# The tail of a ReLU-mean kernel: other column pieces, a third partial sum, and waits in another order

## The chip, the cores and the metric

One core of one Trainium2 chip runs the program. The metric is the time of one execution in device microseconds, the lower the better. Times are medians of several executions of the same program; the profile is of one execution, and its span, from the first to the last instruction, is about 1.3 us shorter than the timed run.

## The reference

```python
x = randn(32, 512, 1024) as float32
out = mean(maximum(x, 0), axis=-1)        # (32, 512) float32
```

That is 16,384 rows of 1024 numbers: 67 MB to read, 64 KB to write. ReLU with a sum along the row is one instruction per 128 rows on either VectorE or ScalarE.

## The kernel before

All loads are issued by SyncE, in the order in which they are used. The first 128 rows go apart, then 7 loads of 8 MB rotate through three buffers, then come row pieces of 7, 4, 2 and 1 rows per partition. The very last row of each partition is cut into column pieces, so that work on it can start before all of it is there. The two helpers are one instruction each in the program; in the profile each shows as an operation followed by a read of the accumulator.

```python
def act_row(nc, src, acc):                       # ScalarE
    return nc.scalar.activation(out=src, in_=src, func=ACT.Relu, accum_out=acc)

def dve_row(nc, src, acc, init=None):            # VectorE
    return nc.vector.tensor_scalar(out=src, in0=src, scalar1=0.0, scalar2=init,
                                   op0=ALU.max, op1=ALU.add, accum_out=acc)
# ...
    col_pieces = [512, 256, 256]
    last = sbuf("last", P, D + 2)                # the last row, and two partial sums behind it
    scale = sbuf("scale", P, D // 4 + 2)         # filled with 1/D
# ...
    nc.scalar.wait_ge(loaded[i + 1], 16)         # first piece
    act_row(nc, last[:, :512], last[:, D:D + 1]).then_inc(act, 1)
    nc.vector.wait_ge(loaded[i + 2], 16)         # second piece
    dve_row(nc, last[:, 512:768], last[:, D + 1:D + 2]).then_inc(dve, 1)
    nc.vector.wait_ge(act, n_done + 1)
    nc.vector.wait_ge(dve, n_done + 1)
    nc.vector.wait_ge(loaded[i + 3], 16)         # third piece
    nc.vector.scalar_tensor_tensor(              # "the final operation"
        out=last[:, 768:], in0=last[:, 768:], scalar=0.0, in1=scale[:, :],
        op0=ALU.max, op1=ALU.mult, accum_out=res[:, J - 1:J],
    ).then_inc(dve, 1)

    nc.sync.wait_ge(pool, 2)
    nc.sync.wait_ge(dve, n_done + 2)
    nc.sync.dma_start(out=outr, in_=res[:, :]).then_inc(stored, 16)   # "the store"
```

The final operation reads the third piece and, in the same pass, the two partial sums that stand behind it in memory. A partial sum is never negative, so the ReLU leaves it alone, and one multiplication by 1/D and one accumulation give the mean. It therefore waits for three things: the third load, ScalarE's count and VectorE's own count.

In the built program each of these instructions carries one wait. Where there are more, the others go to an EventSemaphore instruction set ahead of it, which holds up to two. Which wait goes where follows from the order of the calls. With two or three waits the one called first stays in the instruction, and those called later go to the EventSemaphore, the last call at its head. For the final operation above this gives [third load, VectorE] in the EventSemaphore and ScalarE in the instruction.

## Time and profile before

| | before |
|---|---|
| median of 3 runs, then of 6 | 161.53 us, 161.47 us (161.30 to 161.75) |
| packets of the load queue, share of 16 engines' span | 97.7% |
| VectorE busy, ScalarE busy | 46%, 44% |
| final operation starts, after the last count of the third load | 0.240 us |
| store starts, after the last count of the third load | 0.750 us |
| last count of the store, after its start | 1.639 us |

The first rows say that the kernel is a stream of loads with two engines that keep up easily. The last three say what is not covered by the stream: the tail. The last rows are worked out from the semaphore records in the trace, which hold the time of each increment. A load or store raises its semaphore in 16 steps of one; "landed" is the last of the 16. An engine's count is the increment that an operation makes at its end.

### The profile page before, as it was taken

The numbers are of one execution on the slowest core, as the hardware profiler recorded it, in microseconds if no ns is written. First come the engines' busy times: TensorE is split into PE (matmuls) and PEld (weight loads), VectorE is DVE, ScalarE is ACT, GpSimd is POOL, SyncE is SP. The second block draws the span as 40 slices with busy tenths as digits, with TensorE's granted clock in tenths as the row PEclk, the third lists the DMA queues.
The fourth block names the chain that finished last, engine by engine and source line by source line (L and its number), as shares of the span: only waits on it lengthen the run. The fifth ranks groups of instructions, "written<-read, shape, count | busy, mean of one in ns | idle before, by whom it ended". The sixth has DMA issues, their size and how long they took to land. (4 is left out here: it accounts for less than half of the span.)

```text
span 160.2 us, 347 instructions
## 1 busy us (share of the span) xinstructions
DVE 73.3 (46%) x131; ACT 70.4 (44%) x133; POOL 1.3 (1%) x9
## 2 busy tenths in 40 slices
DVE  0000029900498006960079500993009920299984
ACT  1400029800496006950079300991009900299983
POOL 1000000000000000000000000000000000000001
DMA  9969969979989899699699699699699797998992
GB/s 393 507 278 523 507 278 523 442 344 523 409 376 523 360 425 524 294 491 523 262 524 523 262 523 524 262 523 523 262 524 458 327 523 327 425 451 367 419 412 102
DMA packets 2312, 67.18 MB, mean 419 GB/s; under 512 B 392, under 2 KB 648, under 8 KB 1032
## 3 DMA queue, kind: packets, MB, share of 16 engines
q1 hardware_dynamic: 2312, 67.18, 97.7%
HBM read 67.11 MB, written 0.07 MB: 419 GB/s over the span
## 5 line engine op out<-in xcount | busy, mean ns | idle before, releaser
L20 DVE TENSOR_SCALAR_CACHE_REDUCE rows<-rows 128x1024 f32<-128x1024 f32 (+1 forms) x63 | 72.1, 1208 | 78.9 <-DMA rows<-in_x_dram 78.7
L15 ACT ACTIVATE rows<-rows 128x1024 f32<-128x1024 f32 x64 | 66.2, 1035 | 84.1 <-DMA rows<-in_x_dram 83.9
L15 ACT ACTIVATION_READ_ACCUMULATOR rows<-rows 128x1 f32 x64 | 11.9, 186 | 0.0
L20 DVE DVE_READ_ACCUMULATOR rows<-rows 128x1 f32 x63 | 5.2, 82 | 0.0
L168 DVE STREAM_TRANSPOSE turned<-mean 128x32 f32<-128x32 f32 x1 | 0.2, 213 | 5.9 <-ACT row L164 5.9
L164 ACT ACT_TABLE_LOAD x1 | 1.3, 1283 | 3.3 <-DMA row<-in_x_dram 3.3
L157 POOL TENSOR_SCALAR res<-sums 128x112 f32<-128x112 f32 (+1 forms) x2 | 0.5, 250 | 154.0 <-DVE rows L20 154.0
L164 ACT ACTIVATE row<-row 128x1024 f32<-128x1024 f32 x1 | 1.1, 1056 | 0.0
L15 ACT ACTIVATE last<-last 128x512 f32<-128x512 f32 x1 | 0.6, 630 | 0.0
L20 DVE TENSOR_SCALAR_CACHE_REDUCE last<-last 128x256 f32<-128x256 f32 x1 | 0.4, 420 | 0.3 <-DMA last<-in_x_dram 0.3
L197 DVE SCALAR_TENSOR_TENSOR last<-last,scale 128x258 f32<-128x258 f32 x1 | 0.4, 428 | 0.1
L142 POOL MEMSET scale<- 128x258 f32 x1 | 0.3, 314 | 0.0
L187 POOL TENSOR_SCALAR res<-part 128x1 f32<-128x1 f32 x1 | 0.3, 267 | 0.6 <-DVE rows L20 0.6
L164 ACT ACTIVATION_READ_ACCUMULATOR row<-row 128x1 f32 x1 | 0.2, 186 | 0.0
L15 ACT ACTIVATION_READ_ACCUMULATOR last<-last 128x1 f32 x1 | 0.2, 186 | 0.0
L141 POOL MEMSET mean<- 128x32 f32 x1 | 0.1, 126 | 1.5 <-POOLq L55 1.5
L232 POOL MEMSET const-uint8-127<- 128x1 uint8 x1 | 0.1, 103 | 0.0
L232 POOL MEMSET const-bfloat16-1.0<- 128x1 bf16 x1 | 0.1, 102 | 0.0
L232 POOL MEMSET const-float32-0.0<- 128x1 f32 x1 | 0.1, 99 | 0.2 <-issue 0.2
L232 POOL MEMSET const-float32-1.0<- 128x1 f32 x1 | 0.1, 99 | 0.0
L20 DVE DVE_READ_ACCUMULATOR last<-last 128x1 f32 x1 | 0.1, 83 | 0.0
L197 DVE DVE_READ_ACCUMULATOR last<-last,scale 128x1 f32 x1 | 0.1, 82 | 0.0
## 6 DMA issues: line engine op xcount, KB each, us to landing
rows<-in_x_dram SPq DMA_DIRECT2D x1, 3584.0 KB, 38.1
rows<-in_x_dram SPq DMA_DIRECT2D x1, 2048.0 KB, 42.6
rows<-in_x_dram SPq DMA_DIRECT2D x1, 1024.0 KB, 44.7
row<-in_x_dram SPq DMA_DIRECT2D x1, 512.0 KB, 3.3
rows<-in_x_dram SPq DMA_DIRECT2D x1, 512.0 KB, 45.4
last<-in_x_dram SPq DMA_DIRECT2D x1, 256.0 KB, 45.6
last<-in_x_dram SPq DMA_DIRECT2D x2, 128.0 KB, 45.4
rows<-in_x_dram SPq DMA_DIRECT2D x7, 48.8
```

The costliest lines, as they stand in the source:

```text
L15: return nc.scalar.activation(out=src, in_=src, func=ACT.Relu, accum_out=acc)
L20: return nc.vector.tensor_scalar(out=src, in0=src, scalar1=0.0, scalar2=init, op0=ALU.max, op1=ALU.add, accum_out=acc,)
L141: nc.gpsimd.memset(mean0[:, :], 0.0)
L142: nc.gpsimd.memset(scale[:, :], inv).then_inc(pool, 1)
L157: nc.gpsimd.tensor_scalar(out=res[:, lo:hi], in0=sums[:, lo:hi], scalar1=inv, scalar2=0.0, op0=ALU.mult, op1=ALU.add,)
L164: nc.scalar.activation(out=row0[:, :], in_=row0[:, :], func=ACT.Relu, scale=inv, accum_out=mean0[:, 0:1],).then_inc(first, 1)
L168: nc.vector.transpose(turned0[:, :], mean0[:, :]).then_inc(first, 1)
L187: nc.gpsimd.tensor_scalar(out=res[:, J - 2:J - 1], in0=part[:, 0:1], scalar1=part[:, 1:2], scalar2=inv, op0=ALU.add, op1=ALU.mult,).then_i ...
L197: nc.vector.scalar_tensor_tensor(out=last[:, 768:], in0=last[:, 768:], scalar=0.0, in1=scale[:, :], op0=ALU.max, op1=ALU.mult, accum_out=r ...
L232: nc = _bacc.Bacc("TRN2", target_bir_lowering=False, num_devices=1)
```

## The change

Its intent has two parts. VectorE sat idle for 0.29 us between the row before and the second piece; by making the first piece larger (576) and the second smaller (192), and giving VectorE 128 columns of the first, it is to work in that time and be done sooner. And the wait that passes last is to stand in the instruction itself, so that no EventSemaphore has to run after it.

```diff
-    col_pieces = [512, 256, 256]
+    col_pieces = [576, 192, 256]
-    last = sbuf("last", P, D + 2)
-    scale = sbuf("scale", P, D // 4 + 2)
+    last = sbuf("last", P, D + 3)
+    scale = sbuf("scale", P, D // 4 + 3)
...
-    act_row(nc, last[:, :512], last[:, D:D + 1]).then_inc(act, 1)
+    act_row(nc, last[:, :448], last[:, D:D + 1]).then_inc(act, 1)
+    nc.vector.wait_ge(loaded[i + 1], 16)
+    dve_row(nc, last[:, 448:576], last[:, D + 1:D + 2])
     nc.vector.wait_ge(loaded[i + 2], 16)
-    dve_row(nc, last[:, 512:768], last[:, D + 1:D + 2]).then_inc(dve, 1)
-    nc.vector.wait_ge(act, n_done + 1)
+    dve_row(nc, last[:, 576:768], last[:, D + 2:D + 3]).then_inc(dve, 1)
     nc.vector.wait_ge(dve, n_done + 1)
     nc.vector.wait_ge(loaded[i + 3], 16)
+    nc.vector.wait_ge(act, n_done + 1)
     nc.vector.scalar_tensor_tensor(
...
+    nc.sync.wait_ge(dve, n_done + 2)
     nc.sync.wait_ge(pool, 2)
-    nc.sync.wait_ge(dve, n_done + 2)
     nc.sync.dma_start(out=outr, in_=res[:, :]).then_inc(stored, 16)
```

In the built program the final operation now has [ScalarE, third load] in its EventSemaphore, and VectorE's own count in the instruction. The store has GpSimd's count in the EventSemaphore and the final operation's count in itself.

## The prediction

> **What bounds the kernel now.** I read the page's slices first, then the chain that ended last, then the timeline of the last four microseconds, then short windows over its DMA.
>
> ```profile
> span 160.2 us, 347 instructions
> DVE 73.3 (46%) x131; ACT 70.4 (44%) x133; POOL 1.3 (1%) x9
> DMA  9969969979989899699699699699699797998992
> q1 hardware_dynamic: 2312, 67.18, 97.7%
> ```
>
> The queue's packets fill 97.7% of what 16 engines had; VectorE and ScalarE work under half of the span. The body is the load of 67 MB and nothing in the diff touches its size or the seven large loads. Only the tail after the last bytes can change, and the chain that ended last sees only that tail:
>
> ```profile
> 157.97 0.09 issue
> 158.06 0.12 DVE last L197
> 158.18 0.24 issue
> 158.41 0.08 DVE last L197
> ```
>
> L197 is the final operation on VectorE, and ahead of it stand 0.09 us in which nothing works. The timeline (start, length, engine, line) tells how the tail got there:
>
> ```profile
> 156.49 0.58 ACT L15 ACTIVATE rows<-rows 128x448 f32<-128x448 f32 x1
> 156.49 0.75 DVE L20 TENSOR_SCALAR_CACHE_REDUCE rows<-rows 128x576 f32<-128x576 f32 x1
> 157.16 0.63 ACT L15 ACTIVATE last<-last 128x512 f32<-128x512 f32 x1
> 157.17 0.08 DVE L20 DVE_READ_ACCUMULATOR rows<-rows 128x1 f32 x1
> 157.54 0.42 DVE L20 TENSOR_SCALAR_CACHE_REDUCE last<-last 128x256 f32<-128x256 f32 x1 [0.29 <-DMA last<-in_x_dram]
> 157.70 0.19 ACT L15 ACTIVATION_READ_ACCUMULATOR last<-last 128x1 f32 x1
> 157.89 0.08 DVE L20 DVE_READ_ACCUMULATOR last<-last 128x1 f32 x1
> 158.06 0.43 DVE L197 SCALAR_TENSOR_TENSOR last<-last,scale 128x258 f32<-128x258 f32 x1
> 158.41 0.08 DVE L197 DVE_READ_ACCUMULATOR last<-last,scale 128x1 f32 x1
> 158.57 0.35 SPq L205 DMA_DIRECT2D out_dram<-res  x1
> ```
>
> VectorE waits 0.29 us for the second piece, works until 157.97, and the final operation starts at 158.06. The windows (last two columns: DMA share and GB/s) show that the last bytes move before 157.4:
>
> ```profile
> 157.10:157.20 0.10, 0.10 (x2) 0.09 (x2) 0.00 (x0) 1.00 0.49 164
> ...
> 157.30:157.40 0.10, 0.00 (x0) 0.10 (x1) 0.00 (x0) 1.00 0.04 10
> 157.40:157.50 0.10, 0.00 (x0) 0.10 (x1) 0.08 (x1) 1.00 0.00 0
> ```
>
> The trace's semaphore records give the rest. The last of the 16 counts of the three pieces came at 157.143, 157.518 and 157.820 us; the final operation waits for the third piece (157.820), ScalarE's count (157.896) and VectorE's own (157.981). So VectorE's own middle operation is what passes last, with ScalarE 0.085 and the data 0.16 us earlier. The output store waits for the final operation's count (158.507) and GpSimd's (157.699, long past). From the store's start at 158.57 to its last count at 160.209 it is 1.64 us of transfer, which no part of the change touches; the 1.3 us by which the timed run exceeds the span are not touched either.
>
> **What the Trainium skill says, and whether the trace agrees.** (1) "Perfetto Trace Analysis", section "Identifying Dependency Chains": an instruction with several waits may get an EventSemaphore instruction placed before it that holds the others. Agrees: the built program of before has one ahead of L197 that holds the third load and VectorE's own count, leaving ScalarE's in the instruction; the trace shows it starting at 157.848 for 168 ns. One also stands ahead of the store. (2) The same page, "Per-instruction lifecycle": a VectorE or ScalarE instruction waits in a hardware queue already decoded, while a sequencer-only one must run before the next is decoded. Agrees: where the wait is in the instruction, the start follows the last count by 24 ns (157.518 to 157.542, VectorE) or 22 to 23 ns (157.143 to 157.165, ScalarE). Where VectorE's last wait is in the EventSemaphore it follows by 79 ns (157.981 to 158.060). On SyncE the store follows by 63 ns (158.507 to 158.570): 17 until the EventSemaphore, 17 in it, 29 to the store. (3) The same page, "Optimizing Scalar/DVE Operations": about 60 ns of access overhead per VectorE instruction in engine-busy time. Nearly: start to accumulator read took 344 ns for 256 columns, of which 256 columns at the slope below are 267, so 77 remain. (4) "DMA: Bandwidth & Descriptors", section "How a descriptor splits into AXI transactions": a 256-byte-aligned descriptor goes in 256-byte transactions. The new pieces are 2304, 768 and 1024 bytes at offsets 0, 2304 and 3072, all multiples of 256, so I expect no leftover transaction; no run has shown it yet.
>
> **The change, part by part.**
>
> *The loads.* In the trace a packet of 2048 bytes takes 84 ns and one of 1024 bytes 46, so 38 ns per 1024 bytes and 8 fixed. An estimate from that for 2304 bytes is 93.5, for 768 it is 36.5. Each of 16 engines moves 8 rows of a piece: the first piece lands 8 x 9.5 = 76 ns later (157.219), the second unchanged, because 93.5 + 36.5 = 84 + 46 (157.518), the third unchanged (157.820).
>
> *ScalarE.* It started the 512 columns 22 ns after landing, so data-bound. Now 157.219 + 0.022 = 157.241. From start to accumulator read took 483 ns for 448 columns (156.488 to 156.971, trace) and 536 for 512. With 186 ns of accumulator read and 9 to the count: 157.241 + 0.483 + 0.186 + 0.009 = 157.919, against 157.896 before. So ScalarE ends 23 ns **later**, though it has 64 columns less: the later landing costs more than these save.
>
> *VectorE, the added 128 columns.* Slope: (754 - 420) / (576 - 256) = 1.04 ns per column. So 128 columns take 287 ns, of which 344 - 133 = 211 pass before the accumulator read, where the next operation may already start (the timeline shows 1024-column operations starting together with the read of the one before). It starts at 157.219 + 0.024 = 157.243, and VectorE is free for its successor at 157.454. It lies wholly in the idle 0.29 us, with 0.09 us to spare, and costs the path nothing.
>
> *VectorE, the middle piece.* It starts with the second landing as before, 157.542; 64 columns less are 67 ns off its count: 157.981 - 0.067 = 157.914.
>
> *The final operation.* The EventSemaphore now holds ScalarE's count and the third load, and VectorE's own count is in the instruction. By VectorE alone the start would be 157.914 + 0.024 = 157.938, a gain of 122 ns. But ScalarE's count, at 157.919, passes through the EventSemaphore: 157.919 + 0.079 = 157.998. The later of the two holds: **62 ns gained**, half of what the intent promises. One column more in it is 1 ns.
>
> *The store.* With GpSimd's count in the EventSemaphore (past) and VectorE's in the store itself, I put 17 ns where 63 were: **46 ns gained**. This is the least sure term, because no store in the trace waits this way; 17 ns is what SyncE's EventSemaphores take after their count.
>
> Sum: 62 - 1 + 46 = 107 ns, span 160.24 to 160.14, time 161.53 - 0.11 = **161.42 us**. That is 0.07%.
>
> **The rivals.** *A: VectorE's own count passes last, as the change intends.* That needs ScalarE's count before 157.859 (157.938 - 0.079), 60 ns earlier than I work out; it would gain 122 + 46 = 0.17 us, 161.36. Against it: the larger first piece. *B: a collision.* If the first piece lands over 0.09 us later than I estimate, the 128 columns delay the middle operation and ScalarE alike, and the wait for the new landing eats the gain: nothing from the final operation, 46 ns from the store, 161.48. For it: landings of one piece are spread over 0.28 to 0.33 us across engines; against it: packet times are steady (46 to 59 ns). *C: the store takes its time after the wait, whatever holds the wait* (the descriptors are prepared only then): only 62 ns, 161.47. *D: nothing seen, since runs differ by more.* The three runs before span 161.30 to 161.62, three times the gain; a run's time then says little and only the tail of the trace can tell. I hold D for certain in part: any of A to C may show as anything between -0.3 and +0.1 us.
>
> **Range and chances.** The centre is 161.42. The mechanisms spread from 161.36 (A) to 161.53 (all eaten); the runs scatter by about 0.16 to either side of their median. Together: 161.2 to 161.65, 8 times in 10. Faster by 2% would need 3.2 us, more than the whole tail from the last landing (157.82) to the end of the span (2.4 us), so 0.005. Slower by 2% would need the large loads to be disturbed: 0.005. Within 2%: 0.99.
>
> **What would show each step.** Loads: packets of 2304 and 768 bytes with 93 and 37 ns; first piece's last count some 76 ns nearer to the second's. ScalarE: 448 columns starting about 22 ns after the first landing. VectorE: 128 columns in the former idle time and the middle operation still started by its data; if its idle time before is nil, B holds. Final operation: its start minus ScalarE's count near 79 ns (mine), or its start minus VectorE's count near 24 ns (A). Store: start minus the final count near 17 ns (mine) or 63 (C). I am wrong if the span falls by over 0.2 us, if it grows, or if the body moves the time by more than the tail does.

## The result

The changed kernel took 161.47 us (median of 6 runs, 161.31 to 161.76), the one before 161.47 us (6 runs, 161.30 to 161.75). The ratio is 1.0000, with a 95% interval of 0.9987 to 1.0012: the same.

The profiled run of the changed kernel happens to be the slowest of its six (161.76 us). Its page first; the lines answer to those of before, in the same order.

```profile
span 160.4 us, 349 instructions
DVE 73.5 (46%) x133; ACT 70.3 (44%) x133; POOL 1.3 (1%) x9
DMA  9979979989989799699699699699898998999992
q1 hardware_dynamic: 2312, 67.18, 97.6%
```

Two instructions more on VectorE are the 128-column operation and its accumulator read. The queue is as full as before, with the same packets and bytes.

The end of the chain that ended last (start, length, what; DVEq is VectorE's sequencer, where an EventSemaphore runs):

```profile
157.95 0.20 ACT last L15
158.15 0.03 issue
158.17 0.05 DVEq L198
158.22 0.04 issue
158.27 0.12 DVE last L199
158.38 0.24 issue
158.62 0.08 DVE last L199
```

Before, the chain reached the final operation from VectorE. Now it comes from ScalarE, and passes through an EventSemaphore (L198): 0.03 + 0.05 + 0.04 us lie between ScalarE's end and the final operation. The timeline of the tail (one line of GpSimd and two accumulator reads left out):

```profile
157.47 0.58 ACT L15 ACTIVATE last<-last 128x448 f32<-128x448 f32 x1
157.47 0.29 DVE L20 TENSOR_SCALAR_CACHE_REDUCE last<-last 128x128 f32<-128x128 f32 x1
157.68 0.08 DVE L20 DVE_READ_ACCUMULATOR last<-last 128x1 f32 x1
157.73 0.35 DVE L20 TENSOR_SCALAR_CACHE_REDUCE last<-last 128x192 f32<-128x192 f32 x1
158.01 0.08 DVE L20 DVE_READ_ACCUMULATOR last<-last 128x1 f32 x1
158.27 0.43 DVE L199 SCALAR_TENSOR_TENSOR last<-last,scale 128x259 f32<-128x259 f32 x1 [0.17 <-ACT last L15]
158.73 0.35 SPq L207 DMA_DIRECT2D out_dram<-res  x1
```

VectorE's idle time before the second piece is gone, as intended. It has come back in another place: 0.17 us before the final operation, waiting for ScalarE, where 0.09 us stood before. The windows over the last loads:

```profile
157.50:157.60 0.10, 0.10 (x1) 0.10 (x1) 0.00 (x0) 1.00 0.07 21
157.60:157.70 0.10, 0.10 (x2) 0.10 (x1) 0.07 (x1) 1.00 0.00 0
```

In this run the last bytes move before 157.6, some 0.2 us later than in the profile of before. The change does not make it so: in the two later traces of the changed kernel the last packet ended at 157.16 and 157.20 us, against 157.38 in the profile of before and 157.57 here. The two tails must therefore be compared from the landing of the third piece on. Times in ns, from the semaphore records of the two traces:

| from | to | before | after |
|---|---|---|---|
| first piece landed | third piece landed | 677 | 584 |
| first piece landed | ScalarE's count | 753 | 700 |
| second piece landed | VectorE's own count | 463 | 397 |
| ScalarE's count | final operation starts | 164 | 121 |
| VectorE's own count | final operation starts | 79 | 162 |
| third piece landed | final operation starts | 240 | 237 |
| final operation starts | its count | 447 | 449 |
| final operation's count | store starts | 63 | 17 |
| third piece landed | store starts | 750 | 703 |

So the tail up to the store is 47 ns shorter, which is 46 for the store's own wait and 3 for the final operation's start, less 2 that the operation takes longer. 47 ns are 0.03% of the time, a quarter of the interval's half width.

### The profile page after: what moved, and what is told of

Its sections match the earlier page's. It is cut to its first block, busy times and chain, and to the rows that moved or that the text cites. A ratio compares the mean times of both kernels' runs of the same rounds, so it can differ in the third digit from the quotient of the medians.

```text
span 160.4 us, 349 instructions
## 1 busy us (share of the span) xinstructions
DVE 73.5 (46%) x133; ACT 70.3 (44%) x133; POOL 1.3 (1%) x9
## 3 DMA queue, kind: packets, MB, share of 16 engines
q1 hardware_dynamic: 2312, 67.18, 97.6%
## 4 chain that ended last, share of the span: by engine, by line
DMA 84%; DVE 12%; SPq 1%; issue 1%; ACT 0%; DVEq 0%
DMA rows<-in_x_dram 56%; DMA last<-in_x_dram 29%; DVE rows L20 11%; SPq L109 1%; ACT last L15 0%; DVE last L199 0%; DVEq L198 0%; SPq L115 0%
## 5 line engine op out<-in xcount | busy, mean ns | idle before, releaser
L15 ACT ACTIVATE last<-last 128x448 f32<-128x448 f32 x1 | 0.6, 577 | 0.1
L20 DVE TENSOR_SCALAR_CACHE_REDUCE last<-last 128x128 f32<-128x128 f32 (+1 forms) x2 | 0.6, 321 | 0.0
```

## The experiments

The theory, formed on the table above and called O in the expectations: an EventSemaphore tests its waits one after the other. In the changed kernel ScalarE's count passes last and stands at its head, so the third load's wait is still to be tested after it, though it had passed 116 ns earlier. That makes 121 ns of what I had put at 79. The rival, called Q: ScalarE's count is simply slower to be seen by VectorE than VectorE's own.

### ScalarE's count second in the EventSemaphore

```diff
     nc.vector.wait_ge(dve, n_done + 1)
-    nc.vector.wait_ge(loaded[i + 3], 16)
     nc.vector.wait_ge(act, n_done + 1)
+    nc.vector.wait_ge(loaded[i + 3], 16)
```

> The changed kernel, with the EventSemaphore ahead of the final operation holding the third load first and ScalarE's count second (in the change it is the other way round). Theory O (an EventSemaphore tests its waits one after the other, and a wait behind the one that passes last costs its test again even if long past): from ScalarE's count to the start of the final operation about 79 ns as in the kernel before, where the last to pass stood second, not the 121 ns of the changed kernel; the EventSemaphore ends about 35 ns after the count. Rival Q (ScalarE's count is slower to be seen by VectorE than VectorE's own): still about 121 ns. The time of one run says nothing, 161.3 to 161.8 us under both.

One run, 161.42 us. The end of its chain:

```profile
157.70 0.20 ACT last L15
157.90 0.04 DVEq L198
157.93 0.04 issue
157.98 0.12 DVE last L199
```

The EventSemaphore ended 35 ns after ScalarE's count and the final operation started 80 ns after it. Rival Q falls: the same count, of the same engine, is seen in 80 ns when it stands second and in 121 when it stands first. The final operation started 192 ns after the third landing, against 237.

The EventSemaphore's own record says the same. In this run and in the profile of before it started 28 ns after the third load, the first of its waits, had landed, and ended 35 ns after its second wait had passed (119 and 168 ns later). In the changed kernel it started 26 ns after ScalarE's count, ran 50 ns, and the final operation followed 45 ns after its end: 121.

### ScalarE's count in the instruction

```diff
-    nc.vector.wait_ge(dve, n_done + 1)
-    nc.vector.wait_ge(loaded[i + 3], 16)
     nc.vector.wait_ge(act, n_done + 1)
+    nc.vector.wait_ge(dve, n_done + 1)
+    nc.vector.wait_ge(loaded[i + 3], 16)
```

> The changed kernel with the order of waits at the final operation as before: the third load and VectorE's own count in the EventSemaphore, ScalarE's count in the instruction. Theory O: the instruction starts 79 ns after VectorE's own count or 24 ns after ScalarE's, whichever is later; with the counts as in the changed kernel (ScalarE's 41 ns after VectorE's) both fall within 15 ns of each other, and the start is some 65 to 85 ns after ScalarE's count less the 41, about 38 ns after it. Rival Q (a slow ScalarE count): 60 ns or more after ScalarE's count. One time: 161.3 to 161.8 us under both.

One run, 161.32 us. The start came 79 ns after VectorE's own count, which stood second in the EventSemaphore, and 56 ns after ScalarE's; the two counts were 23 ns apart here and not 41, so 56 where the text names 38. That is only 4 ns short of what rival Q asked for, so this run alone would not decide against it. The start was 188 ns after the third landing: for the new pieces the order of before is better than that of the change.

### The store's waits alone

```diff
-    nc.sync.wait_ge(pool, 2)
     nc.sync.wait_ge(dve, n_done + 2)
+    nc.sync.wait_ge(pool, 2)
```

(on the kernel before)

> The kernel before with only the two waits of the output store exchanged. Theory: from the final operation's count to the store's start 17 ns instead of 63, the store's own 348 ns and its 0.85 us to the first written packet the same, so 46 ns gained and the rest of the tail as before (final operation 79 ns after VectorE's own count). Rival C (the store needs its time behind its wait whatever holds it): the store starts sooner, but its first packet keeps its distance of 0.91 us from the final count. One time: 161.3 to 161.8 us.

One run, 161.55 us. From the final count to the store 17 ns, and from there to the first written packet 844 ns (848 before), so 861 from the final count against 911. The gain at the store is real and stays; rival C falls. The rest of the tail was as before: 79 ns after VectorE's own count. The final operation started 262 ns after the third landing here and 240 in the profile of before, with the same instructions: the spacing of the landings varies from run to run (from the first to the third it was 677, 652 and 624 ns in the three traces with the old pieces), and a gain of a few tens of ns can be read only from the gap between a count and what it releases.

### The orders of waits alone

```diff
-    nc.vector.wait_ge(act, n_done + 1)
     nc.vector.wait_ge(dve, n_done + 1)
     nc.vector.wait_ge(loaded[i + 3], 16)
+    nc.vector.wait_ge(act, n_done + 1)
...
-    nc.sync.wait_ge(pool, 2)
     nc.sync.wait_ge(dve, n_done + 2)
+    nc.sync.wait_ge(pool, 2)
```

(on the kernel before, with its pieces of 512, 256 and 256)

> The kernel before with both reorderings of waits, and the pieces of 512, 256 and 256 kept. There ScalarE's count comes some 85 ns before VectorE's own. Theory O: the start of the final operation is the later of ScalarE's count + 121 ns and VectorE's count + 24 ns, so about 36 ns after VectorE's own count instead of 79; 43 ns gained there and 46 at the store. If the wait in the EventSemaphore cost only 79 ns, the start would be 24 ns after VectorE's count. If reordering gained nothing at the final operation, 79 ns. One time: 161.2 to 161.7 us.

The start came 122 ns after ScalarE's count: the theory's 121. But the number written down, 36 ns after VectorE's own count, was missed: it was 106. The two counts were 16 ns apart in this run and not 85, because the second piece landed 308 ns after the first and not 375. So with the old pieces too, the new order can cost more than it saves, by how the landings fall: 79 ns after VectorE's own count, as before, would have been 27 ns sooner here (an estimate). The time of this run, 162.07 us, is no sign of that: its store took 2.073 us from its start to its last count, where the other eleven traces have 1.58 to 1.88.

### Waits that have long passed, set behind the last one

```diff
     nc.vector.wait_ge(dve, n_done + 1)
-    nc.vector.wait_ge(loaded[i + 3], 16)
+    nc.vector.wait_ge(loaded[0], 16)
+    nc.vector.wait_ge(loaded[1], 16)
     nc.vector.wait_ge(act, n_done + 1)
+    nc.vector.wait_ge(loaded[2], 16)
+    nc.vector.wait_ge(loaded[i + 3], 16)
```

This builds three EventSemaphores: ScalarE's count alone, then two pairs of waits that have all passed.

> The changed kernel with three further waits at the final operation, for loads 0, 1 and 2, passed over 70 us before. They are so placed that ScalarE's count stands alone in a first EventSemaphore and two more EventSemaphores with two long-passed waits each stand between it and the final operation. Theory O (every wait that stands behind the last one to pass costs its test, passed or not, about 33 ns, and each further EventSemaphore its own dispatch): from ScalarE's count to the start 180 to 280 ns instead of 121. Rival (waits that have passed cost nothing, the 121 ns have another cause): 80 to 125 ns. Time of one run: 161.3 to 161.9 us.

One run, 161.44 us. Its chain:

```profile
157.48 0.20 ACT last L15
157.67 0.03 issue
157.70 0.02 DVEq L199
157.72 0.05 issue
157.77 0.05 DVEq L200
157.82 0.05 issue
157.87 0.05 DVEq L201
157.91 0.04 issue
157.96 0.12 DVE last L202
```

From ScalarE's count to the start 288 ns, a little over the 280 that I had as the upper end, and far from the rival's 80 to 125. The lines give the price list. An EventSemaphore with one wait runs 21 ns, one with two passed waits 50 and 49 ns (the trace's own durations), so a wait that has passed costs some 29 ns (an estimate, their difference), and each further EventSemaphore with its dispatch 98 ns (157.768 to 157.866). Waits are cheap only when they are tested before the one that passes last.

### The pieces alone

```diff
-    nc.vector.wait_ge(dve, n_done + 1)
-    nc.vector.wait_ge(loaded[i + 3], 16)
     nc.vector.wait_ge(act, n_done + 1)
+    nc.vector.wait_ge(dve, n_done + 1)
+    nc.vector.wait_ge(loaded[i + 3], 16)
...
-    nc.sync.wait_ge(dve, n_done + 2)
     nc.sync.wait_ge(pool, 2)
+    nc.sync.wait_ge(dve, n_done + 2)
```

(the changed kernel with both orders of before)

> The kernel before with only the pieces of 576, 192 and 256, the third partial sum and the split between ScalarE and VectorE changed; both orders of waits as before. If the pieces are what gains at the final operation and its reordering gives that back: the start 79 ns after VectorE's own count and 185 to 195 ns after the third load's last count, against 240 to 262 before and 237 in the changed kernel; the store 63 ns after the final count. If the pieces gain nothing: 235 ns or more. Time of one run: 161.3 to 161.8 us.

One run, 161.29 us. The start came 78 ns after VectorE's own count and 197 after the third landing (2 ns above the range I gave), the store 63 ns after the final count. So the pieces alone gain 43 ns against the profile of before (240), 65 against the other trace with the same final operation (262); both are single traces and hold the scatter of the landings. In the three traces of the changed kernel the distance is 237, 233 and 254: the new order at the final operation gives about as much back as the pieces gain.

### A version meant to beat both, and the changed kernel again

```diff
-    act_row(nc, last[:, :448], last[:, D:D + 1]).then_inc(act, 1)
+    act_row(nc, last[:, :384], last[:, D:D + 1]).then_inc(act, 1)
-    dve_row(nc, last[:, 448:576], last[:, D + 1:D + 2])
+    dve_row(nc, last[:, 384:576], last[:, D + 1:D + 2])
...
     nc.vector.wait_ge(dve, n_done + 1)
-    nc.vector.wait_ge(loaded[i + 3], 16)
     nc.vector.wait_ge(act, n_done + 1)
+    nc.vector.wait_ge(loaded[i + 3], 16)
```

> A version meant to beat both: the changed kernel with ScalarE's count second in the EventSemaphore, and ScalarE taking 384 columns of the first piece and VectorE 192. ScalarE's count then comes 53 ns sooner, VectorE's own about 10 to 15 ns later, so that neither is last by much. Expected: start 130 to 150 ns after the third load's last count (237 in the changed kernel, 192 with the order alone exchanged), the store 17 ns after the final count; from the last packet of the loads to the store about 1.08 us against 1.16 in the changed kernel and 1.19 before. That is 0.12 us against before, 0.07%: timed ratio 0.9993, which five rounds with an interval like the last one's, 0.12% to either side, will hardly tell from 1.

Beside it ran the changed kernel as it is:

> The changed kernel unchanged, for a second trace of it and a second set of times. Theory: ScalarE's count to the final operation 121 ns again, the final count to the store 17 ns, from the last load packet to the store 1.15 to 1.17 us. Expected time ratio 0.9997, interval holding 1. If the change really costs or gains more than its tail shows, the ratio leaves 0.9985 to 1.0010.

| | runs | median us | ratio to before | 95% interval | final operation after third landing | store after third landing |
|---|---|---|---|---|---|---|
| 384 columns | 6 | 161.33 (161.10 to 161.82) | 0.9993 | 0.9976 to 1.0009 | 150 ns | 615 ns |
| changed, again | 5 | 161.54 (161.29 to 162.04) | 1.0012 | 0.9995 to 1.0029 | 233 ns | 699 ns |

The traces did what was expected: 79 ns after ScalarE's count in the one, 121 in the other, 17 at the store in both (16 in the second). One term was missed: with 384 columns VectorE's own count came 427 ns after the second landing and not 397, so 30 ns later where 10 to 15 were expected. Its second operation was no longer started by the data but by the end of the longer one before it: it started at 157.404 us, together with that one's accumulator read, 58 ns after its data. The ratio of the changed kernel was over the bound of 1.0010 that I had set:

> The changed kernel once more, because its ratio in the last rounds, 1.0012 with an interval of 0.9995 to 1.0029, was over the bound of 1.0010 that was set for it. If that came from scatter (one of five runs at 162.04 us), the ratio is again between 0.9985 and 1.0012 with 1 in its interval. If the change costs time outside its tail, the ratio is again over 1.0010, and the interval lies above 1. The trace again: 121 ns, 17 ns, and 1.15 to 1.18 us from the last load packet to the store.

> The version with 384 columns on ScalarE and its count second, once more, beside the changed kernel on the same chip. Its tail was 0.084 us shorter than the changed kernel's up to the store (1.090 against 1.174 us from the last load packet). If that reaches the time: a ratio 0.0005 below the changed kernel's of these rounds; the interval will be some 0.0015 to either side, so that only an agreement of sign can be asked for. In the trace: start 130 to 160 ns after the third load's last count, store 1.08 to 1.10 us after the last load packet.

| | runs | median us | ratio to before | 95% interval | final operation after third landing | store after third landing |
|---|---|---|---|---|---|---|
| changed, third time | 5 | 161.47 (161.28 to 161.54) | 0.9997 | 0.9984 to 1.0010 | 254 ns | 719 ns |
| 384 columns, again | 6 | 161.31 (161.13 to 161.74) | 0.9993 | 0.9979 to 1.0007 | 157 ns | 624 ns |

The excess did not return, and the bound had been narrower than the interval of five runs; I take it for scatter. The third trace was at 1.195 us from the last load packet to the store, over the 1.15 to 1.18 us that I wrote, while its fixed gaps (122 and 17 ns) were as expected; again the landings differ. The version with 384 columns had the lowest median both times and 0.9993 both times, where 0.12 us would be 0.9993 too; in the second rounds that is 0.0004 below the changed kernel, where 0.0005 was expected. Its shorter tail is shown by both traces; that it shortens the time is not, since both intervals hold 1.

Where the scatter of the times comes from can be read from the twelve traces. The last packet of the loads ended between 157.08 and 157.57 us from the span's start, and the store took between 1.58 and 2.07 us from its start to its last count. Each of the two spreads by 0.49 us (the store by 0.30 without the one run of 2.07), six to ten times what the change gains in its tail, and neither lies in the part that the change moves.

## Why the prediction was right or wrong

- **The bound.** Right. The loads' share stayed (97.7 to 97.6%), and the change moved only the tail. The time, 161.47 us, lies 0.05 us from the forecast, but that is less than the scatter and proves none of the steps; rivals B and C had named 161.48 and 161.47. The forecast gain of 0.11 us did not show: the medians are equal, and an interval of 0.2 us to either side could not have shown it. The trace has to decide.
- **The loads.** Right in the cost. Packets of 2304 and 768 bytes took 93 and 36 ns in the trace (medians), where 93.5 and 36.5 were estimated, and no extra cost of a leftover transaction shows. The landings were forecast from one trace, and it lay high: the first piece landed 584 ns before the third, where 677 - 76 = 601 was forecast, and came 113 ns nearer to the second, where 76 were named as the sign. Over all traces (three with the old pieces, nine with the new) the means are 651 and 580 ns to the third, and 352 and 267 to the second, so 71 and 85 ns nearer.
- **ScalarE.** Right to the nanosecond: its count came 700 ns after the first landing, and 157.919 - 157.219 is 700. It passes last, as worked out, but 41 ns behind VectorE's own count and not 5 (157.919 - 157.914), since the second piece landed sooner after the first than forecast.
- **VectorE.** Right: the accumulator read of the 128 columns came 212 ns after their start (211 forecast), the operation lay in the former idle time, and its successor was still started by its data. The own count came 397 ns after the second landing (396). The collision of rival B did not happen.
- **The final operation.** This is the step that failed: "But ScalarE's count, at 157.919, passes through the EventSemaphore: 157.919 + 0.079 = 157.998." The 79 ns were those of the kernel before, where the last to pass stood second in the EventSemaphore. At its head it takes 121 ns (121, 121 and 122 in three traces of the changed kernel, 122 with the old pieces, 79 to 80 as soon as it is set second). So 42 of the 62 ns were lost there, and 17 to the first and third landing, which were that much closer than estimated; 3 ns remained.
- **The store.** Right: 17 ns instead of 63, and the first packet 848 ns after its start as before, so rival C is out. It was called the least sure term and was the only one that arrived whole.
- **The sum.** 3 - 2 + 46 = 47 ns instead of 62 - 1 + 46 = 107: the final operation itself took 2 ns more and not 1. The other two traces of the changed kernel reach the store 699 and 719 ns after the third landing, so 51 and 31 ns sooner than the 750 of before. Rival A (VectorE last, 0.17 us) is out: no trace of the changed kernel had ScalarE's count early enough. Rival D, that scatter hides it all in the time, holds.

The expected gain of the first part of the change was therefore real and was spent by the second: the pieces make ScalarE last, and the reordering, made for VectorE being last, puts ScalarE's count where a late wait costs most.

What stays open: in three runs VectorE's own count came last while it was held in the instruction (by 16 ns with the old pieces, by 22 in both traces with 384 columns), but each time the EventSemaphore ahead of it ended later still and decided the start. So the 24 ns assumed for a start by VectorE's own count are measured only for loads.

## What to carry to other kernels

Before reordering waits, write down from the trace when each of them passes after the change, not before it: a change that moves work between engines also changes which wait is last. If the last to pass can't be the one in the instruction, it should be the last one tested in the EventSemaphore (79 to 80 ns to the start here, against 121 to 122). A distance between two landings that is read from one trace is a sample: the 677 ns used here lay 26 over the mean of three traces. When the stream of loads scatters by ten times the gain, judge a tail by the gap between a count and what it releases; sixteen timed runs of the changed kernel did not tell here what one trace of each variant did.

## What the Trainium skill lacked or had wrong

- "Perfetto Trace Analysis", section "Identifying Dependency Chains", says that EventSemaphore instructions may be inserted for further waits, but not that their waits are tested in order, nor the cost. Here, from the last count to the start on VectorE: 23 to 24 ns with the wait in the instruction (a load), 78 to 80 ns with it second of two in an EventSemaphore, 121 to 122 ns with it first of two; each further EventSemaphore of two passed waits added 98 ns.
- The same page, section "Per-instruction lifecycle", shows the wait of a DMA issue after its decoding, without numbers. The runs agree with it: a store on SyncE started 16 to 17 ns after its count with the wait in itself, 63 ns with an EventSemaphore before it, and its own 347 to 348 ns and the 0.84 to 0.85 us to its first packet were the same.
- "Advanced Engine Details and Errata", section "Network/Comms", gives 50 to 100 ns for reading a semaphore value from a sequencer. If that is the same act as testing a wait that has passed, these runs show less: an EventSemaphore with two such waits ran 49 to 50 ns, one with a single wait 21.
- The pages on DMA and on traces give no figure for how far the 16 counts of one load are spread. In the kernel before, those of the last three pieces came over 0.28 to 0.33 us each (0.37 to 0.89 in the other eleven traces), and the last of all 0.44 us after the last packet had ended (0.45 to 0.48).
